# Moving the weight splits of a mixture-of-experts gate/up stage into the branch that uses them

## The chip, the cores and the metric

The kernel runs on one core of a Trainium2 chip. The metric is the device time of one execution in microseconds (us), the median of three runs. The engines are TensorE (PE in the profile; PEld is its weight load), VectorE (DVE), ScalarE (ACT), GpSimd (POOL) and SyncE (SP), whose queue issues most of the transfers from HBM.

## The reference

Two decoder layers over 256 tokens of width 1024. Each has a mixer (sparse attention, a convolution and a state-space group), a feed-forward part and a gated per-layer embedding. The feed-forward part of the second layer is the one that the change touches: eight experts, of which every token takes two.

```
def swiglu(x, w1, w3, w2):
    return (jax.nn.silu(x @ w1) * (x @ w3)) @ w2

def moe_swiglu(x, router, w1, w3, w2):
    logits = (x @ router).astype(jnp.float32)
    top_vals, top_idx = lax.top_k(logits, TOP_K)
    wts = jax.nn.softmax(top_vals, axis=-1)
    comb = jnp.einsum('blk,blke->ble', wts, jax.nn.one_hot(top_idx, N_EXPERTS, dtype=jnp.float32))
    y = jnp.zeros(x.shape, jnp.float32)
    for e in range(N_EXPERTS):
        y = y + comb[..., e:e + 1] * swiglu(x, w1[e], w3[e], w2[e])
    return y.astype(x.dtype)
```

w1 and w3 of an expert are 1024 x 3584, w2 is 3584 x 1024, all float32.

## The kernel before

The kernel computes only the tokens that an expert was given. `gather` collects them into `xe`, `expert` runs the three matrix products, and the result is scattered back (`sc`) and added to `y`. The 3584 columns are taken in four **chunks** (three of 1024, one of 512). An expert needs 42 loads of 1 MB each: 28 for w1 and w3 (eight per chunk of 1024, four for the last chunk) and 14 for w2, the down product. All loads of all experts stand in one list; `feed` issues the next one on SP's queue (L269) as soon as one of 13 buffers of 1 MB is free, so a transfer starts when the reader of an earlier load has let go of its buffer.

How many tokens an expert got is known only when the kernel runs. `either` therefore writes each load's matmuls twice, in two arms of an If on the count `n`:

```
            with self.tc.If(n > SM) as many:
                emit(False)
            with many.Else():
                emit(True)
            self.give()
        self.flush()
```

SM is 64. In the arm for at most 64 tokens (called **few** here) PE multiplies the raw float32 weights (L1537), with two halves of the columns in two halves of the array. In the other arm (**many**) each product is made of three faster matmuls (`mm3`, L334 to L336) from a high and a low part of the weights: ScalarE writes the high part (`split`, L339), VectorE the rest (L340), two pairs of instructions per load, into four buffers `whl`. These splits stand ahead of the If, in `split = list(self.parts(w, ku, cw))`, whatever the arm. For w2 both arms use the raw weights (L1573) and there is no split. `n` is loaded into a register of PE alone, so PE alone takes the branch; on the other engines each If is an empty block.

After a chunk `gate` follows: ScalarE's Silu of the first product (`hb`, L1496), VectorE's product with the second (`hb`, L1497), then PE's transposes (`hT`, L1507) and two copies out of PSUM (`ht`: ScalarE L1516, VectorE L1514). `flush` writes each of these steps behind a later load's If. VectorE also zeroes the halves of new accumulators (`mgu`, L1484). A scheduler then fixes the order on each engine, and may put whole Ifs of the next expert among those of this one's down product; every engine meets the Ifs in one and the same order.

Of the kernel before, what the change touches and what calls it, by code (L numbers as in the profile page):

```python
# [17 lines left out]
S = 256  # L18
# [136 lines left out]
RBN = 2  # L155
OV = 2
HB = 4
LOADS = 42
SM = 64
OVF = 6  # L160
# [33 lines left out]
class Trunk:  # L194
# [64 lines left out]
    def feed(self):  # L259


        while self.slots and self.nspec < len(self.specs):
            pool, tag, n = slot = self.slots.pop(0)
            if slot == self.over and OVF * LOADS <= self.nspec and self.kept is not None:
                self.kept.append(slot)
            elif pool is not self.xp or self.nspec < (NE - 1) * LOADS:
                src, a, b = self.specs[self.nspec]
# [21 lines left out]
    def parts(self, raw, a, b, low=None):  # L289
# [3 lines left out]
        for i0 in range(0, a, step):  # L293
            m = min(step, a - i0)
            n = m * b
            flat = raw[:, i0 : i0 + m].rearrange("p a b -> p (a b)")
            both = self.st.tile([P, 2, 1024], F32R, tag="hl", name="whl", bufs=HB)
            hi, lo = both[:, 0, :n], both[:, 1, :n]
# [269 lines left out]
    def square_parts(self, order, raw, low):  # L568
# [3 lines left out]
        for n, k in enumerate(order):  # L572
            if n % 2 == 0:
                both = self.st.tile([P, 2, D], F32R, tag="hl", name="whi", bufs=HB)
            hi = both[:, n % 2]
# [20 lines left out]
    def mixer(self, l, mp):  # L596
# [17 lines left out]
        def kv_columns():  # L614
# [8 lines left out]
            for ku in range(4):  # L623
                if ku == 2:
                    yield kv
                for kk, wh, wl in self.stream(w[:, 2 * ku : 2 * ku + 2, 512:1304], 2, 792):
# [3 lines left out]
                    if late:  # L630

                        held.append((k, wh, wl))
                        if k < HB - 1:
                            continue
# [651 lines left out]
    def moe(self, l, mp):  # L1286
        nc, a, sm = self.nc, self.a, self.sm
# [80 lines left out]
        cint = mp.tile([1, 1 + NE], I32, name="cint")  # L1368
# [20 lines left out]
        def pair(e):  # L1389

            advance(self.gather(th, tl, [one_hot(e, tt) for tt in range(TT)], S, GT))

        for e in range(NE):
            if e == OVF:

                while self.todo:
                    self.flush()
                self.ring, self.nload = self.kept, 0
                self.overflow(j, mp, Da[:, e // 2 % 2], cint, th, tl, rank, sel, comb, y)
                self.slots, self.kept = self.slots + self.kept, None  # L1400
                self.feed()
                pair(e)
            Dm = Da[:, e // 2 % 2]
            es = ts(e % 2)
            De = [Dm[:, tt, e % 2] for tt in range(TT)]
            D2 = mp.tile([P, TT, P], F32, tag="D2", name="D2")
            for tt in range(TT):
                nc.vector.tensor_scalar(D2[:, tt], slots, rank2[:, tt, e : e + 1], sel[:, tt, e : e + 1], op0=ALU.is_equal, op1=ALU.mult)
            ce = [comb[:, tt, e : e + 1] for tt in range(TT)]
            n = nc.tensor.value_load(cint[0:1, e + 1 : e + 2], min_val=0, max_val=S)  # L1410
            ahead = (lambda: pair(e + 1)) if e % 2 and e + 1 not in (OVF, NE) else None
            last = e == NE - 1
            late = self.ple_early(l, mp) if last else None
            self.expert(mp, None, n, self.xh[:, :, es], De, [D2[:, tt] for tt in range(TT)], ce, y, ahead, norm if last else None, late)
            if e == NE - 2:

                lnp = self.ln_params(l, 1, mp, "tl")
                bias = self.ple_bias(l, mp.tile([P, D], F32, tag="h2", name="gb"), mp.tile([P, D], F32R, tag="th", name="gbr"))
# [51 lines left out]
    def expert(self, mp, loads, n, xe, Dm, D2, comb, y, ahead=None, done=None, late=None):  # L1470
# [3 lines left out]
        nc = self.nc  # L1474
# [5 lines left out]
        def pair(name):  # L1480
            acc = self.pair(name)
            if n is not None:
                for h in range(2):
                    nc.vector.memset(acc[h][rows[1 - h]], 0.0)  # L1484
            return acc
# [6 lines left out]
        def gate(ci, hw, accs):  # L1492
            hbs = []
            for h in range(2):
                hb = mp.tile([P, 512], F32, tag="hb", name="hb", bufs=2)
                nc.scalar.activation(hb[:, :hw], accs[0][h][:, :hw], AF.Silu)  # L1496
                nc.vector.tensor_mul(hb[:, :hw], hb[:, :hw], accs[1][h][:, :hw])  # L1497
                hbs.append(hb)
            self.todo.append(lambda: turn(ci, hw, hbs))
# [22 lines left out]
        for ci, (c0, cw) in enumerate(CHUNKS):  # L1522
            hw, ku = cw // 2, 2048 // cw
            accs = []
            for wi in range(2):
                acc = pair("mgu")
                for u in range(KT // ku):
                    w = get()
                    split = list(self.parts(w, ku, cw))

                    def emit(few):
                        for i, wh, wl in split:
                            k = u * ku + i
                            for h in range(2):
                                hs = slice(h * hw, (h + 1) * hw)
                                if few:
                                    mm(acc[h][rows[h], :hw], xe[:, k, 0:SM], w[:, i, hs], start=k == 0, stop=k == KT - 1)  # L1537
                                else:
                                    self.mm3(acc[h][:, :hw], xs[:, 0, k], xs[:, 1, k], wh[:, hs], wl[:, hs], k == 0, k == KT - 1)

                    self.either(n, emit)
                accs.append(acc)
            if ci == 0:

                def turn_slots():

                    ps = self.tr("DT")
                    for i, src in enumerate([v.bitcast(F32) for v in Dm] + D2):
                        nc.tensor.transpose(ps[:, i * P : (i + 1) * P], src, self.ident)

                    def out():
                        t = mp.tile([P, 2, TT, P], F32R, tag="DT", name="DT", bufs=1)
                        nc.scalar.activation(t.rearrange("p h t s -> p (h t s)"), ps, AF.Copy)
                        DT.append(t)

                    self.todo.append(out)

                self.todo.append(turn_slots)
            self.todo.append(lambda ci=ci, hw=hw, accs=accs: gate(ci, hw, accs))
        acc = pair("mo")  # L1560
        NK = D_FFE // P
        for g in range(NK // 2):
            if late:
                next(late, None)
            w = get()

            def emit(few):
                for i in range(2):
                    k = 2 * g + i
                    ht, hf = hts[k]  # L1570
                    for h in range(2):
                        dst, x = (acc[h][rows[h]], ht[:, rows[hf]]) if few else (acc[h], ht)
                        mm(dst, x, w[:, i, h * 512 : (h + 1) * 512], start=k == 0, stop=k == NK - 1)  # L1573

            self.either(n, emit)
            if g == 3 and ahead:
                ahead()
# [202 lines left out]
```

## Time and profile before

| | us |
|---|---|
| time, median of 3 runs (lowest, highest) | 1639.78 (1639.73, 1644.44) |
| the profiled execution's own time | 1649.05 |
| its span, first to last instruction | 1647.3 |
| in it: eight experts, 629.7 to 1605.9 | 976.2 |

The page gives the busy time of each engine over the whole span: PE 1433.5 us (87%), VectorE 1195.0 us (73%), ScalarE 859.8 us (52%). These shares are means over stages with different limits, so what counts here is read expert by expert.

### The profile page before, as it was taken

Reading aid. Unit: us, or ns where it says so; the run is one execution under the profiler, and the core shown is the slowest. Engines: PE = TensorE matmul, PEld = TensorE weight load, DVE = VectorE, ACT = ScalarE, POOL = GpSimd, SP = SyncE. Lnnn points to the kernel's source line nnn. Section 1 sums busy time; section 2 is a strip of 40 time slices with the busy share of each in tenths; the row PEclk is TensorE's granted clock in tenths of the full one; section 3 lists DMA queues with packets and bytes.
Section 4 is the critical chain, followed back from the end, with each engine's and each line's share of the span. In section 5 each row is a group of like instructions: output and inputs, shape, how many; then the busy total and the mean of one; then the engine's idle time right before and its main releaser. Section 6 shows DMA issues by size and latency. Waiting matters only on the chain. (4 is left out here: it accounts for less than half of the span.)

```text
span 1647.3 us, 19143 instructions
## 1 busy us (share of the span) xinstructions
PE 1433.5 (87%) x6702; PEld 900.9 (55%) x6703; DVE 1195.0 (73%) x1564; ACT 859.8 (52%) x1175; POOL 261.4 (16%) x202
## 2 busy tenths in 40 slices
PE   6776999998987787798799998799999998688797
PEld 6544788876764473242347833347756843233245
DVE  7989558647679868968848837859736906967956
ACT  5454455434464536846536535647535705755742
POOL 4755107503044401000000000000000000001030
PEclk9797999999997798889899999899999999789898
DMA  6431465553542166999999989999979996999971
GB/s 244 150 132 39 155 202 184 172 191 134 179 136 102 51 249 262 370 365 409 404 342 404 364 283 381 361 351 405 374 268 352 368 309 241 352 372 394 402 315 51
DMA packets 139649, 445.56 MB, mean 270 GB/s; under 512 B 7408, under 2 KB 19312, under 8 KB 138496
## 3 DMA queue, kind: packets, MB, share of 16 engines
q1 hardware_dynamic: 138496, 437.42, 71.8%
q0 software_dynamic: 1024, 6.38, 1.1%
q8 instruction: 86, 1.41, 0.3%
q14 instruction: 43, 0.35, 0.1%
HBM read 442.72 MB, written 1.05 MB: 269 GB/s over the span
## 5 line engine op out<-in xcount | busy, mean ns | idle before, releaser
L340 DVE TENSOR_TENSOR whl<-wraw,whl 128x1024 fp32r<-128x1024 f32 (+2 forms) x557 | 661.2, 1227 | 178.0 <-ACT whl L339 173.4
L339 ACT ACTIVATE whl<-wraw 128x1024 fp32r<-128x1024 f32 (+2 forms) x557 | 565.1, 1041 | 312.8 <-DMA wraw<-in_moe_w_dram 73.2
L1537 PE MATMUL mgu<-wraw,xe 128*64 128x512 f32 (+1 forms) x1280 | 276.7, 583 | 13.3 <-DMA wraw<-in_moe_w_dram 5.5
L1573 PE MATMUL mo<-wraw,ht 128*64 128x512 f32 (+1 forms) x896 | 276.5, 598 | 0.0
L1537 PEld LDWEIGHTS mgu<-wraw,xe 128*64 128x64 f32 x1280 | 98.3, 149 | 179.7 <-issue 165.8
L1573 PEld LDWEIGHTS mo<-wraw,ht 128*64 128x64 f32 (+1 forms) x896 | 104.3, 158 | 148.3 <-issue 144.8
L334 PE MATMUL mgu<-whl,xs 128*128 128x512 f32 (+1 forms) x384 | 145.5, 379 | 6.1 <-DVE mgu L1484 5.0
L336 PE MATMUL mgu<-whl,xs 128*128 128x512 f32 (+1 forms) x384 | 140.4, 366 | 0.5 <-DVE whl L340 0.5
L335 PE MATMUL mgu<-whl,xs 128*128 128x512 f32 (+1 forms) x384 | 139.9, 364 | 0.0
L536 POOL DMA_DIRECT2D lnp<-in_lnp_dram x5 | 2.8, 565 | 799.0 <-ACT xe L1446 758.1
L1507 PE MATMUL hT<-sqr,hb 128*128 128x128 f32 x224 | 41.7, 342 | 80.0 <-DVE hb L1497 79.9
L334 PEld LDWEIGHTS mgu<-whl,xs 128*128 128x128 f32 x384 | 72.5, 189 | 27.6 <-DVE mgu L1484 7.5
L1507 PEld LDWEIGHTS hT<-sqr,hb 128*128 128x128 f32 x224 | 33.4, 176 | 97.1 <-ACT whl L339 63.7
L335 PEld LDWEIGHTS mgu<-whl,xs 128*128 128x128 f32 x384 | 72.6, 189 | 13.0 <-issue 1.7
L340 DVE TENSOR_TENSOR ot<-mo,ot 128x512 fp32r<-128x512 f32 x16 | 10.6, 688 | 95.2 <-ACT ot L339 95.1
L336 PEld LDWEIGHTS mgu<-whl,xs 128*128 128x128 f32 x384 | 72.4, 189 | 13.1 <-DVE whl L340 1.0
L1484 DVE MEMSET mgu<- 64x512 f32 x128 | 62.1, 485 | 21.6 <-issue 7.6
L336 PE MATMUL fffn_w<-whl,xh 128*128 128x512 f32 (+1 forms) x192 | 72.1, 375 | 0.0
L335 PE MATMUL fffn_w<-whl,xl 128*128 128x512 f32 (+1 forms) x192 | 71.8, 374 | 0.0
L334 PE MATMUL fffn_w<-whl,xh 128*128 128x512 f32 (+1 forms) x192 | 71.4, 372 | 0.0
L339 ACT ACTIVATE ot<-mo 128x512 fp32r<-128x512 f32 x16 | 9.0, 596 | 113.4 <-PE mo L1573 113.4
L1497 DVE TENSOR_TENSOR hb<-hb,mgu 128x512 f32<-128x512 f32 (+1 forms) x64 | 36.6, 612 | 27.1 <-PE mgu L335 14.8
(374 smaller groups left out, 2358.5 us busy)
## 6 DMA issues: line engine op xcount, KB each, us to landing
wraw<-in_moe_w_dram SPq DMA_DIRECT2D x336, 1024.0 KB, 7.9
wraw<-in_ffn_w_dram SPq DMA_DIRECT2D x33, 1024.0 KB, 5.1
wraw<-in_cmp_w_dram SPq DMA_DIRECT2D x8, 1024.0 KB, 5.4
wraw<-in_w_out_dram SPq DMA_DIRECT2D x8, 1024.0 KB, 7.0
wraw<-in_ple_gate_w_dram SPq DMA_DIRECT2D x8, 1024.0 KB, 7.2
wraw<-in_w_in_dram SPq DMA_DIRECT2D x8, 792.0 KB, 6.3
wraw<-in_w_in_dram SPq DMA_DIRECT2D x8, 768.0 KB, 7.0
lnp<-in_lnp_dram POOLq DMA_DIRECT2D x5, 1024.0 KB, 5.7
```

The source lines that it names most:

```text
L334: mm(dst, xh, wh, start=start, stop=False)
L335: mm(dst, xl, wh, start=False, stop=False)
L336: return mm(dst, xh, wl, start=False, stop=stop)
L339: h = self.hi = self.nc.scalar.activation(dh, src, AF.Copy)
L340: return h, (low or self.nc.vector).tensor_tensor(dl, src, dh.bitcast(F32), op=ALU.subtract)
L536: (queue or self.nc.gpsimd).dma_start(t.rearrange("p a d -> p (a d)"), self.a["lnp"][l, i : i + 1, :].to_broadcast([P, 2 * D]))
L1484: nc.vector.memset(acc[h][rows[1 - h]], 0.0)
L1497: nc.vector.tensor_mul(hb[:, :hw], hb[:, :hw], accs[1][h][:, :hw])
L1507: nc.tensor.transpose(pss[h][:, i * P : (i + 1) * P], hbs[h][:, i * P : (i + 1) * P], self.ident)
L1537: mm(acc[h][rows[h], :hw], xe[:, k, 0:SM], w[:, i, hs], start=k == 0, stop=k == KT - 1)
L1573: mm(dst, x, w[:, i, h * 512 : (h + 1) * 512], start=k == 0, stop=k == NK - 1)
```

## The change

The list of splits ahead of the If goes; `emit` makes the splits itself, in the many arm only. So that ScalarE and VectorE can skip them, the count is loaded into a register of those two engines as well (`values_load` with three engines), and with that every If of every expert, those of the down product too, becomes a compare and a branch on three engines instead of one.

```
+BRANCH = (mybir.EngineType.PE, mybir.EngineType.Activation, mybir.EngineType.DVE)
...
-            n = nc.tensor.value_load(cint[0:1, e + 1 : e + 2], min_val=0, max_val=S)
+            n = nc.values_load(cint[0:1, e + 1 : e + 2], engines=BRANCH, min_val=0, max_val=S)
...
                     w = get()
-                    split = list(self.parts(w, ku, cw))
 
                     def emit(few):
-                        for i, wh, wl in split:
+                        for i, wh, wl in [(i, None, None) for i in range(ku)] if few else self.parts(w, ku, cw):
                             k = u * ku + i
                             for h in range(2):
                                 hs = slice(h * hw, (h + 1) * hw)
```

The lines of the changed kernel stand one higher. The order of instructions moves with it. On ScalarE, at the end of the first chunk of the first expert (the pattern is the same in the other chunks and experts), the splits of the loads that arrive on DMAHW7 and then DMAHW0 stand before the change so:

```order
L339 ACTIVATE whl<-wraw 128x1024 [waits DMAHW7_49,DVE_49,PE_49]
L339 ACTIVATE whl<-wraw 128x1024 [waits DVE_49,PE_49]
L339 ACTIVATE whl<-wraw 128x1024 [waits DMAHW0_49,DVE_49,PE_49]
L339 ACTIVATE whl<-wraw 128x1024 [waits DVE_49,PE_49]
L1463 UNCONDITIONAL_BRANCH
L1516 ACTIVATE ht<-hT 128x512 [waits PE_49]
```

and in the changed kernel so:

```order
L340 ACTIVATE whl<-wraw 128x1024 [waits DVE_49,DMAHW7_49,PE_49,Activation_49]
L340 ACTIVATE whl<-wraw 128x1024
L1464 UNCONDITIONAL_BRANCH
L1464 UNCONDITIONAL_BRANCH [waits Activation_49]
L1517 ACTIVATE ht<-hT 128x512 [waits PE_49]
L1464 COMPARE_AND_BRANCH
L340 ACTIVATE whl<-wraw 128x1024 [waits DMAHW0_49,DVE_49,Activation_49]
L340 ACTIVATE whl<-wraw 128x1024
L1464 UNCONDITIONAL_BRANCH
L1464 UNCONDITIONAL_BRANCH [waits Activation_49]
```

The splits are now framed by a compare-and-branch and two jumps (the second is the few arm, which is empty but for a wait), and the copy `ht`, which waits for PE's transposes, stands ahead of the splits of the load on DMAHW0 instead of behind them. On PE, at the same place, the transposes stand before the change between the loads on DMAHW6 and DMAHW7:

```order
L1537 MATMUL mgu<-wraw,xe 64x512 [waits DMAHW6_49,DVE_49]
L1537 MATMUL mgu<-wraw,xe 64x512 [waits DVE_49]
L1537 MATMUL mgu<-wraw,xe 64x512 x2
L1463 UNCONDITIONAL_BRANCH
L1507 MATMUL hT<-sqr,hb 128x128 [waits DVE_49]
L1507 MATMUL hT<-sqr,hb 128x128 x3
L1507 MATMUL hT<-sqr,hb 128x128 [waits DVE_49,Activation_49]
L1507 MATMUL hT<-sqr,hb 128x128 x3
L1463 COMPARE_AND_BRANCH
```

and in the changed kernel one load later, between DMAHW7 and DMAHW0:

```order
L1537 MATMUL mgu<-wraw,xe 64x512 [waits DMAHW7_49]
L1537 MATMUL mgu<-wraw,xe 64x512 x3
L1464 UNCONDITIONAL_BRANCH
L1508 MATMUL hT<-sqr,hb 128x128 [waits DVE_49]
L1508 MATMUL hT<-sqr,hb 128x128 x3
L1508 MATMUL hT<-sqr,hb 128x128 [waits DVE_49,Activation_49]
L1508 MATMUL hT<-sqr,hb 128x128 x3
L1464 COMPARE_AND_BRANCH
```

Before, the transposes came before the block of the load on DMAHW7 and the copies that read them behind the splits of DMAHW0. After, transposes, copies and the splits of DMAHW0 follow upon one another. VectorE's order, shown here from the changed kernel, has the same sequence with its own work in front (`mgu` are the zeroed halves):

```order
L1498 TENSOR_TENSOR hb<-hb,mgu 128x512 [waits DVE_49,PE_49]
L1485 MEMSET mgu 64x512 [waits DVE_49] x2
L1515 COPY ht<-hT 128x512 [waits PE_49]
L1464 COMPARE_AND_BRANCH
L341 TENSOR_TENSOR whl<-wraw,whl 128x1024 [waits DMAHW0_49,Activation_49]
L341 TENSOR_TENSOR whl<-wraw,whl 128x1024 [waits Activation_49]
L1464 UNCONDITIONAL_BRANCH
L1464 UNCONDITIONAL_BRANCH [waits DVE_49]
```

There too nothing of the load on DMAHW0 is split before the copy `ht` is done.

## Rows read from the trace of the kernel before

**Rows 1.** Busy time and count by line, operation and tile, whole span.
```profile
L340 DVE TENSOR_TENSOR whl<-wraw,whl 128x1024 fp32r<-128x1024 f32 (+2 forms) x557 | 661.2, 1227 | 178.0 <-ACT whl L339 173.4
L339 ACT ACTIVATE whl<-wraw 128x1024 fp32r<-128x1024 f32 (+2 forms) x557 | 565.1, 1041 | 312.8 <-DMA wraw<-in_moe_w_dram 73.2 <-PE mgu L336 60.2 <-PE fffn_w L336 44.9
L1537 PE MATMUL mgu<-wraw,xe 128*64 128x512 f32 (+1 forms) x1280 | 276.7, 583 | 13.3 <-DMA wraw<-in_moe_w_dram 5.5 <-DVE mgu L1484 4.3 <-DVE comb L1330 3.4
...
L336 PE MATMUL mgu<-whl,xs 128*128 128x512 f32 (+1 forms) x384 | 140.4, 366 | 0.5 <-DVE whl L340 0.5
```
**Rows 2.** One stretch per expert: us, busy PE PEld DVE ACT POOL, PEclk, DMA share, GB/s.
```profile
629.70:749.40 119.70, 97.00 (x443) 38.99 (x443) 94.73 (x112) 73.83 (x83) 0.00 (x0) 0.89 0.94 360
749.40:866.30 116.90, 98.85 (x457) 43.92 (x456) 86.72 (x98) 65.44 (x74) 0.00 (x0) 0.93 0.99 384
866.30:999.60 133.30, 130.91 (x522) 85.03 (x522) 86.93 (x99) 66.68 (x72) 0.00 (x0) 0.99 0.96 352
999.60:1113.80 114.20, 96.75 (x457) 43.08 (x457) 86.93 (x99) 65.45 (x74) 0.00 (x0) 0.94 0.96 364
1113.80:1248.10 134.30, 132.12 (x537) 91.25 (x537) 86.28 (x96) 66.99 (x72) 0.00 (x0) 1.00 0.94 348
1248.10:1370.40 122.30, 120.36 (x485) 81.72 (x484) 68.27 (x77) 52.58 (x57) 0.00 (x0) 1.00 0.90 321
1370.40:1503.00 132.60, 102.48 (x476) 44.98 (x477) 102.80 (x116) 79.55 (x89) 2.54 (x4) 0.87 0.93 348
1503.00:1605.90 102.90, 88.10 (x398) 35.32 (x398) 83.13 (x89) 63.76 (x73) 16.89 (x10) 0.93 0.94 369
```
**Rows 3.** PE in order of time, first expert (few): start, us, what, idle before.
```profile
633.68 13.95 PE L1537 MATMUL mgu<-wraw,xe 128*64 128x512 f32 x64
654.39 1.97 PE L1507 MATMUL hT<-sqr,hb 128*128 128x128 f32 x8 [6.76 <-DVE hb L1497]
656.29 14.43 PE L1537 MATMUL mgu<-wraw,xe 128*64 128x512 f32 x64
677.01 1.94 PE L1507 MATMUL hT<-sqr,hb 128*128 128x128 f32 x8 [6.28 <-DVE hb L1497]
```
**Rows 4.** VectorE in order of time, one chunk of the first expert.
```profile
660.18 5.74 DVE L340 TENSOR_TENSOR whl<-wraw,whl 128x1024 fp32r<-128x1024 f32 x5
...
676.19 1.27 DVE L1497 TENSOR_TENSOR hb<-hb,mgu 128x512 f32<-128x512 f32 x2
677.38 3.48 DVE L340 TENSOR_TENSOR whl<-wraw,whl 128x1024 fp32r<-128x1024 f32 x3
680.79 0.68 DVE L1514 COPY ht<-hT 128x512 f32<-128x512 f32 x1
```
**Rows 5.** Stretches of steady work, columns as in rows 2.
```profile
1500.00:1590.00 90.00, 75.67 (x342) 31.45 (x344) 70.48 (x80) 62.06 (x72) 3.42 (x2) 0.92 1.03 404
1110.00:1175.00 65.00, 62.52 (x288) 50.64 (x287) 59.84 (x66) 47.76 (x50) 0.00 (x0) 1.00 1.03 404
...
880.00:926.00 46.00, 46.00 (x210) 37.92 (x210) 44.28 (x47) 36.94 (x39) 0.00 (x0) 1.00 1.02 387
1365.00:1392.00 27.00, 21.27 (x96) 11.95 (x97) 17.79 (x26) 13.20 (x16) 0.60 (x1) 0.87 0.64 229
```
**Rows 6.** DMA issues: size of one, us from issue to landing.
```profile
wraw<-in_moe_w_dram SPq DMA_DIRECT2D x336, 1024.0 KB, 7.9
```
**Rows 7.** PE in order of time, second expert, down product.
```profile
816.61 1.94 PE L1573 MATMUL mo<-wraw,ht 128*64 128x512 f32 x8
...
819.26 1.95 PE L1537 MATMUL mgu<-wraw,xe 128*64 128x256 f32 x16
```
**Rows 8.** ScalarE in order of time, third expert (many).
```profile
904.04 1.06 ACT L339 ACTIVATE whl<-wraw 128x1024 fp32r<-128x1024 f32 x1 [0.31 <-PE mgu L336]
905.42 1.06 ACT L339 ACTIVATE whl<-wraw 128x1024 fp32r<-128x1024 f32 x1 [0.31 <-PE mgu L336]
906.79 1.06 ACT L339 ACTIVATE whl<-wraw 128x1024 fp32r<-128x1024 f32 x1 [0.31 <-PE mgu L336]
907.75 0.58 ACT L1516 ACTIVATE ht<-hT 128x512 f32<-128x512 f32 x1
```
**Rows 9.** PE in order of time, third expert: transposes of two chunks.
```profile
906.59 1.03 PE L1507 MATMUL hT<-sqr,hb 128*128 128x128 f32 x8
929.53 1.03 PE L1507 MATMUL hT<-sqr,hb 128*128 128x128 f32 x8
```

More of the change, by code (lines that the diff above doesn't have):

```diff
@@ L157 @@
 HB = 4
+BRANCH = (mybir.EngineType.PE, mybir.EngineType.Activation, mybir.EngineType.DVE)
 LOADS = 42
@@ L1409, in moe @@
             ce = [comb[:, tt, e : e + 1] for tt in range(TT)]
-            n = nc.tensor.value_load(cint[0:1, e + 1 : e + 2], min_val=0, max_val=S)
+            n = nc.values_load(cint[0:1, e + 1 : e + 2], engines=BRANCH, min_val=0, max_val=S)
             ahead = (lambda: pair(e + 1)) if e % 2 and e + 1 not in (OVF, NE) else None
@@ L1528, in expert @@
                     w = get()
-                    split = list(self.parts(w, ku, cw))
                     def emit(few):
-                        for i, wh, wl in split:
+                        for i, wh, wl in [(i, None, None) for i in range(ku)] if few else self.parts(w, ku, cw):
                             k = u * ku + i
```

## The prediction

> **What bounds the kernel now.** I first read the groups by line, to see how much work the change touches. ScalarE's 557 split instructions take 565.1 us and VectorE's 557 take 661.2 us [rows 1]; both counts hold the 448 of the experts (56 pairs in each of eight) and some of earlier stages. In the few arm these parts are read by nobody: there PE takes the raw weights.
>
> Next come the stretches, one per expert [rows 2]. They show two kinds. In three, the third, fifth and sixth, PE is busy for 130.91 of 133.30 us, 132.12 of 134.30 and 120.36 of 122.30: those are the many arms, and PE's matmuls set the time. In the other five PE is busy for 97 of 120 us or so. Those are the few arms, with a DMA share of 0.93 to 0.99. It would be easy to stop here and call them bound by transfers. But the best steady rate shown is 404 GB/s at a share of 1.03 [rows 5], and the first few expert moved only 360 [rows 2]. So there are gaps, and the order of time must say who makes them.
>
> It does for the first expert. PE runs a chunk's 64 matmuls in 13.95 us without waiting, then stands still for 6.76 us, next time 6.28 us, and the releaser is VectorE's `hb` [rows 3]. VectorE meanwhile runs split behind split, five in 5.74 us, and comes to `hb` when its queue lets it [rows 4]. From transposes to transposes PE needs 677.01 - 654.39 = 22.6 us per chunk. So the gate/up stage of a few expert is held by VectorE, through splits that nobody reads.
>
> What is the next limit? A load is 1024.0 KB [rows 6], 1.0486 million bytes, and at 404 GB/s takes 2.60 us. Eight loads of a chunk take 20.8 us, the 42 of an expert 109.2 us.
>
> **What is removed.** Five few experts lose 5 x 56 = 280 pairs: 280 x 1.041 = 291 us of ScalarE and 280 x 1.227 = 344 us of VectorE, by the means of [rows 1]. Nearly all of that is off the path, since behind VectorE stands the transfer queue. A chunk goes from 22.6 us to the larger of 20.8 (transfers) and PE's 13.95 + 1.97 = 15.9 [rows 3], plus a short wait for the Silu and product, which the pause of PE between loads covers. The gain is 22.6 - 20.8 = 1.8 us a chunk, 3.5 chunks, 6.3 us an expert. The last few expert (102.90 us, and 404 GB/s over most of it [rows 2, 5]) is at the floor already. Four experts give 25 us; as the first chunk partly lives on loads that came early, I take **24**.
>
> Bounds, by the floor: the stretches of 119.7, 116.9, 114.2 and 132.6 us lie 10.5, 7.7, 5.0 and 23.4 above 109.2 [rows 2]. From the last I take off the pause at 1365 to 1392, with 229 GB/s over 27 us [rows 5], 27 x (1 - 229/404) = 11.7, which a check between experts makes. Sum 34.9, so at most **35**. From below: the idle DMA shares are 0.06, 0.01, 0.04 and 0.07 of these stretches [rows 2], 7.2 + 1.2 + 4.6 + 9.3 = 22, less the pause's 0.36 x 27 = 9.7: **12**.
>
> **What is moved.** In the many arms the splits stay, 84 loads, but may no longer run ahead of an If. The chunks of 1024 repeat every 929.53 - 906.59 = 22.94 us [rows 9], 1.03 of it transposes, so a load's matmuls take 21.9 / 8 = 2.74 us. PE is busy in 46.00 of 46.00 us there, VectorE in 44.28 [rows 5], so VectorE has 0.86 us to spare per chunk, no more. ScalarE even waits 0.31 us for PE before each split [rows 8]: it is ahead.
>
> After the change the transposes, the copies `ht` and the splits of the next load stand one behind the other, with no matmuls of PE in between (the order in the section on the change). ScalarE can copy after the first half of the transposes, 0.52 us; its copy takes 0.58 and a split 1.06 [rows 8], so the first high part is there at 2.16, where PE was done at 1.03 [rows 9]: a wait of 1.13. Each of the load's twelve matmuls takes 2.74 / 12 = 0.23 us; PE does the two that need the high part alone, 0.46, until 2.62; the third needs the low part, which VectorE gives at 2.16 + 1.2 = 3.36 [rows 1]: another 0.74. Together 1.9 us per chunk end. The fourth turn lies in the down product, which has no splits, so it is three per expert, nine in all: **17 us** lost. Bounds: if only the high part is missed, 1.13 x 9 = **10**. VectorE's view is worse: it idles from its last low part over PE's last four matmuls (0.92), the transposes (1.03) and from its copy's end (0.68 [rows 4]) to the split at 3.08 (0.45), 2.4 us in all, of which 0.86 is spare. That is 1.5, near the 1.9 of PE, so both engines lose the same time; without the spare, 2.4 x 9 = **22**.
>
> A second order effect I cost at nothing: ScalarE's splits of a load now wait at once for the whole block of PE two loads back, where they waited half by half. The 0.31 us waits show that it has the time, and where it is late the price is in the upper bound.
>
> **What is added.** Each If is a compare and a branch on ScalarE and VectorE. The trace shows no such instruction on them. From below nothing: VectorE's five splits take 1.148 us each across the jumps of empty Ifs [rows 4], and PE, which branches already, needs 1.74 us per load over eight Ifs [rows 3], no more than the 1.94 of a single one [rows 7]. From above I take ScalarE's 0.31 us [rows 8], the nearest pause between two neighbours on such an engine: 84 x 0.31 = 26 us. It is nearest to the jumps and to PE's branch, so I take nothing; VectorE, with the 2.4 us stalls counted, has some 0.04 us per load left as cover in the many arms. In the few arms and in the down products both engines have nothing to do, and transfers hide the branch, as they hide PE's own pauses: PE works 1.94 and 1.95 us on blocks that start 2.65 us apart [rows 7]. The register loads, one per engine and expert, stand where PE waited for the count anyway.
>
> [...]
>
> **Sum.** The profiled run took 1649.05 us for its 1647.3 us span and lies 9.3 us above the median of the runs, 1639.8. 1649.05 - 24 + 17 = 1642; less those 9.3, 1632.8 on the scale of the median. I take **1632**.
>
> **The rivals.**
> *The many arms lose nothing.* If the 13 buffers let a late gate/up stage be made up in the down product, whose blocks of 1.74 to 1.94 us are shorter than a load, only the gain is left: 1639.8 - 24 = 1616, with the floor's 35 it is 1605. For it: the DMA share in many experts is 0.90 to 0.96 [rows 2]. Against it: PE works in 98% of their time, so what it loses has nowhere to be made up.
> *Slower: the branch is exposed on VectorE.* Place: every split load of the many arms. At 0.31 us less 0.04 of cover, 84 x 0.27 = 23 us, and 1632 + 23 = 1655. It decides from (7 / 84) + 0.04 = 0.12 us per branch; from 0.18 the kernel is slower by more than 0.3%. For it: VectorE has 44.28 of 46 us filled [rows 5]. Against it: PE's own branches don't show.
> *Little happens.* The few arms gain only the idle DMA share, 12, and the stalls cost 17: 1639.8 - 12 + 17 = 1645. For it: the second expert already runs at 384 GB/s and a share of 0.99 [rows 2]. Against it: the 6 us waits of every chunk [rows 3].
>
> **How the numbers follow.** 0.3% of 1640 is 4.9 us, about what this measurement can tell from no change. My forecast, 1632 (own range 1624 to 1640), has 0.42; two thirds of it is faster, one third the same. The many arms unhurt: 0.18, all faster. The branch exposed: 0.20, nearly all slower. Little happens: 0.20, half the same, half slower. So faster 0.46, same 0.25, slower 0.29. The range goes from 1608, within the first rival, to 1658, just beyond the second.
>
> **What would show it.** Right: in few experts no PE wait for `hb` of over 2 us, chunks of 20.8 us, 400 GB/s; in many experts a PE wait of 1.1 and then 0.7 us behind `hT` at three chunk ends, chunks of 24.8 us. Wrong, if few stretches stay at 115 to 120 us, if many chunks stay at 22.9, or if each split on VectorE is followed by a pause of 0.1 us or more and PE waits for `whl` at every load.

## The result, and the profile after

The changed kernel takes 1655.26 us (median of four runs, 1654.95 to 1656.19) against 1641.3 beside it: ratio 1.0084, 95% interval 1.0066 to 1.0102. It is 14 us slower, where 8 us faster was forecast (1632 against 1639.8); the time lies inside the stated range, the direction is wrong.

The stretches, cut as in [rows 2] at each expert's last scatter, show both sides at once (columns as there):

```profile
620.80:733.80 113.00, 91.73 (x443) 34.24 (x443) 23.58 (x52) 11.42 (x19) 0.00 (x0) 0.90 0.98 379
733.80:851.50 117.70, 94.99 (x457) 43.03 (x456) 32.92 (x50) 18.15 (x26) 0.00 (x0) 0.91 0.97 377
851.50:995.20 143.70, 134.72 (x521) 86.05 (x521) 77.82 (x91) 56.01 (x64) 0.00 (x0) 0.98 0.89 324
995.20:1105.80 110.60, 92.95 (x457) 41.59 (x456) 33.16 (x51) 18.15 (x26) 0.00 (x0) 0.94 0.98 378
1105.80:1254.70 148.90, 140.08 (x536) 95.23 (x536) 86.57 (x96) 64.02 (x73) 0.00 (x0) 0.95 0.86 313
1254.70:1388.90 134.20, 125.81 (x484) 83.95 (x484) 73.34 (x81) 53.86 (x61) 0.00 (x0) 0.97 0.84 301
1388.90:1512.40 123.50, 96.53 (x477) 40.13 (x477) 26.09 (x48) 12.28 (x21) 2.54 (x4) 0.88 0.98 378
1512.40:1612.50 100.10, 82.05 (x398) 33.73 (x398) 34.37 (x45) 20.45 (x29) 16.88 (x10) 0.93 0.95 374
```

Line by line against [rows 2], the five few experts change by -6.7, +0.8, -3.6, -9.1 and -2.8 us, together -21.4. The three many experts change by +10.4, +14.6 and +11.9, together +36.9. VectorE is indeed relieved, from 94.73 to 23.58 us busy in the first expert, and still the stage is 15.5 us longer. Two more things are to be seen in the many lines: PE is idle for 8 to 9 us of each where it was idle for about 2, and its granted clock, 0.99 and twice 1.00 before, is 0.98, 0.95 and 0.97.

A little is gained ahead of these stretches, which begin with the first expert's first matmul. From the router's first product (`lg`) to that matmul the kernel before takes 23.9 us (605.78 to 629.71) and the changed one 21.3 (599.50 to 620.78). The other kernels below with the splits ahead of the If take 23.6 to 24.0 us there, those with the splits in the arm 21.0 to 21.3. With these 2.6 us the balance is 36.9 - 21.4 - 2.6 = 12.9, near the 14 of the medians.

PE in order of time at one chunk end of the third expert, which answers to [rows 9], shows both:

```profile
899.33 1.03 PE L1508 MATMUL hT<-sqr,hb 128*128 128x128 f32 x8
901.62 0.50 PE L335 MATMUL mgu<-whl,xs 128*128 128x512 f32 x1 [1.25 <-ACT whl L340]
901.96 0.39 PE L336 MATMUL mgu<-whl,xs 128*128 128x512 f32 x1
902.88 0.50 PE L337 MATMUL mgu<-whl,xs 128*128 128x512 f32 x1 [0.53 <-DVE whl L341]
...
903.73 0.63 PE L337 MATMUL mgu<-whl,xs 128*128 128x512 f32 x1
904.16 0.63 PE L335 MATMUL mgu<-whl,xs 128*128 128x512 f32 x1
...
906.72 0.54 PE L335 MATMUL mgu<-whl,xs 128*128 128x512 f32 x1
907.10 0.39 PE L336 MATMUL mgu<-whl,xs 128*128 128x512 f32 x1
```

The two waits behind the transposes are there as forecast, 1.25 for ScalarE and 0.53 for VectorE. What was not forecast stands below them: from 903.73 the matmuls follow at 0.43 us instead of 0.23 until 907.1. That is half speed: the granted clock of this stretch is 0.50, where from 899 to 903 us it was 1.00:

```profile
904.00:907.00 3.00, 3.00 (x8) 2.33 (x8) 2.23 (x2) 0.41 (x1) 0.00 (x0) 0.50 0.04 10
```

ScalarE and VectorE at the same place:

```profile
900.03 0.60 ACT L1517 ACTIVATE ht<-hT 128x512 f32<-128x512 f32 x1 [3.93 <-PE hT L1508]
900.52 3.89 ACT L340 ACTIVATE whl<-wraw 128x1024 fp32r<-128x1024 f32 x4
907.01 2.01 ACT L340 ACTIVATE whl<-wraw 128x1024 fp32r<-128x1024 f32 x2 [2.60 <-PE mgu L337]
```
```profile
900.40 0.69 DVE L1515 COPY ht<-hT 128x512 f32<-128x512 f32 x1 [0.83 <-PE hT L1508]
901.60 4.63 DVE L341 TENSOR_TENSOR whl<-wraw,whl 128x1024 fp32r<-128x1024 f32 x4 [0.50 <-ACT whl L340]
```

ScalarE idles 3.93 us until the transposes let its copy go, and only then comes to the splits that PE waits for. Further waits of this kind stand at the start of the same expert, behind the last scatter, and in mid-chunk:

```profile
853.10 0.50 PE L335 MATMUL mgu<-whl,xs 128*128 128x512 f32 x1 [1.63 <-ACT whl L340]
856.02 0.79 PE L337 MATMUL mgu<-whl,xs 128*128 128x512 f32 x1 [2.18 <-DVE whl L341]
916.03 0.50 PE L337 MATMUL mgu<-whl,xs 128*128 128x512 f32 x1 [0.28 <-DVE whl L341]
```

At the start ScalarE's first split begins at 852.00, behind its copy `DT`, which waits for the scatter. In the kernel before the first blocks were split earlier: there ScalarE's next split stands only at 870.76. Behind the third chunk there is no such wait. Its transposes stand behind the last matmul of gate/up, and the down product that follows needs no splits; so the order shown for the first chunk is not the same in every chunk:

```profile
930.81 1.04 PE L1508 MATMUL hT<-sqr,hb 128*128 128x128 f32 x8
```

The groups of PE by line for the third expert (busy, mean ns, idle before) add the waits up, of after and then of before:

```profile
L335 PE MATMUL mgu<-whl,xs 128*128 128x512 f32 (+1 forms) x112 | 41.9, 376 | 4.1 <-ACT whl L340 4.1
L337 PE MATMUL mgu<-whl,xs 128*128 128x512 f32 (+1 forms) x112 | 41.9, 380 | 4.3 <-DVE whl L341 4.3
```
```profile
L334 PE MATMUL mgu<-whl,xs 128*128 128x512 f32 (+1 forms) x112 | 41.9, 374 | 1.8 <-DVE mgu L1484 1.8
L336 PE MATMUL mgu<-whl,xs 128*128 128x512 f32 (+1 forms) x112 | 40.8, 364 | 0.0
```

8.4 us of waits against 1.8; the other two many experts have 8.2 and 8.1 against 1.6 each. So waits explain 24.7 - 5.0 = 19.7 of the 36.9 us. In the third expert they are 3.8 us at the start (1.8 before), 3.5 at the two chunk ends and 1.1 in mid-chunk. Most of the other 17 is half speed: the clock's shortfall, 0.02 x 143.7 + 0.05 x 148.9 + 0.03 x 134.2 less the 0.01 x 133.3 of before, comes to about 13 us.

### The profile page after: what moved, and what is told of

The parts are those of the page before. It is cut to its first block, busy times and chain, and to the rows that moved or that the text cites. A ratio compares the mean times of both kernels' runs of the same rounds, so it can differ in the third digit from the quotient of the medians.

```text
span 1652.7 us, 19521 instructions
## 1 busy us (share of the span) xinstructions
PE 1417.1 (86%) x6702; PEld 888.8 (54%) x6703; DVE 880.2 (53%) x1284; ACT 576.0 (35%) x895; POOL 261.4 (16%) x202
## 5 line engine op out<-in xcount | busy, mean ns | idle before, releaser
L341 DVE TENSOR_TENSOR whl<-wraw,whl 128x1024 fp32r<-128x1024 f32 (+2 forms) x277 | 334.3, 1237 | 184.2 <-ACT whl L340 183.2
L340 ACT ACTIVATE whl<-wraw 128x1024 fp32r<-128x1024 f32 (+2 forms) x277 | 275.1, 1029 | 247.3 <-DMA wraw<-in_moe_w_dram 55.5
L1537 PE MATMUL mgu<-wraw,xe 128*64 128x512 f32 (+1 forms) x1280 | 256.0, 549 | 48.2 <-DMA wraw<-in_moe_w_dram 41.1
L1537 PEld LDWEIGHTS mgu<-wraw,xe 128*64 128x64 f32 x1280 | 92.5, 138 | 200.3 <-issue 134.9
L335 PE MATMUL mgu<-whl,xs 128*128 128x512 f32 (+1 forms) x384 | 150.1, 392 | 44.9 <-ACT whl L340 44.9
L337 PE MATMUL mgu<-whl,xs 128*128 128x512 f32 (+1 forms) x384 | 147.0, 388 | 12.5 <-DVE whl L341 12.4
L336 PE MATMUL mgu<-whl,xs 128*128 128x512 f32 (+1 forms) x384 | 144.8, 379 | 0.0
L335 PEld LDWEIGHTS mgu<-whl,xs 128*128 128x128 f32 x384 | 76.0, 198 | 67.7 <-ACT whl L340 53.3
L1497 ACT ACTIVATE hb<-mgu 128x512 f32<-128x512 f32 (+1 forms) x64 | 33.2, 543 | 191.9 <-PE mgu L1537 162.0
L1517 ACT ACTIVATE ht<-hT 128x512 f32<-128x512 f32 (+1 forms) x32 | 17.4, 544 | 220.2 <-PE hT L1508 220.2
L337 PEld LDWEIGHTS mgu<-whl,xs 128*128 128x128 f32 x384 | 74.7, 197 | 34.2 <-DVE whl L341 21.6
L336 PEld LDWEIGHTS mgu<-whl,xs 128*128 128x128 f32 x384 | 76.0, 198 | 14.1 <-issue 1.7
L984 DVE SCALAR_TENSOR_TENSOR cy<-upad,pk,cy 128x256 f32<-128x256 f32 x60 | 54.7, 912 | 1.1
```

Source lines behind the costliest of these rows:

```text
L335: mm(dst, xh, wh, start=start, stop=False)
L336: mm(dst, xl, wh, start=False, stop=False)
L337: return mm(dst, xh, wl, start=False, stop=stop)
L340: h = self.hi = self.nc.scalar.activation(dh, src, AF.Copy)
L341: return h, (low or self.nc.vector).tensor_tensor(dl, src, dh.bitcast(F32), op=ALU.subtract)
L984: nc.vector.scalar_tensor_tensor(y0, u(0, k), w(0, k), y0, op0=ALU.mult, op1=ALU.add)
```

## The experiments

Theory: the loss is the order of the splits in the many arms, with half-speed matmuls as its consequence; the gain of the few arms is real. Rivals: the branch on ScalarE and VectorE costs the time; the few arms were held by transfers.

**The branch alone.** The changed kernel with the splits put back ahead of the If:

```
                     w = get()
+                    split = list(self.parts(w, ku, cw))
 
                     def emit(few):
-                        for i, wh, wl in [(i, None, None) for i in range(ku)] if few else self.parts(w, ku, cw):
+                        for i, wh, wl in split:
```

> The three engines branch, but the splits stay ahead of the If as before the change. Theory (the loss is the order of the splits in the many arms, and half-speed matmuls after the waits that it makes): nothing is lost, 1637 to 1646 us, as the kernel before. Rival (the branch itself costs time on VectorE and ScalarE): at 0.1 us a branch the 224 split loads, which VectorE has no spare for, add 22 us, 1663; and if the whole loss of the many experts, 37 us in the traces, were the branch, 1678 or more.

Measured: 1643.74 us against 1643.47, ratio 1.0000 (0.9987 to 1.0014). All 336 Ifs (eight experts of 42 loads) branch on three engines and nothing is lost, even in the few chunks where VectorE has no spare (from 655 to 690 us no pause of it is longer than 0.18 us): from transposes to transposes they take 674.60 - 651.99 = 22.61 us, as in [rows 3].

```profile
651.99 1.97 PE L1508 MATMUL hT<-sqr,hb 128*128 128x128 f32 x8 [7.79 <-DVE hb L1498]
674.60 1.94 PE L1508 MATMUL hT<-sqr,hb 128*128 128x128 f32 x8 [5.10 <-DVE hb L1498]
```

The branch falls as a cause. In this run the arms of ScalarE and VectorE are empty; where they hold the splits, in the changed kernel, VectorE's four splits of two loads take 4.63 us in the row shown above, 1.16 each as against 1.15 in [rows 4], so the branch between them does not show either. All of the 14 us comes from where the splits stand.

**All experts in one arm.** The condition of the If is replaced, in the kernel before and in the changed one (and with it the threshold up to which an expert's slots are doubled); for all few it is `n > 2 * P`:

```
-            with self.tc.If(n > SM) as many:
+            with self.tc.If(n > 0) as many:
```

> The kernel before with the condition set to n > 0 (and the doubled slots of small experts left out with it), so that all eight experts take the many arm. Only a base for the next run: by the three many experts' stretches, 134.3, 133.3 and 122.3, against 117.3 in the mean of the five others, about 5 x 13 = 65 us over the kernel before, 1705 us.

> The changed kernel with the same condition. Theory (37 us lost in three many experts, 12 each): 8 x 12 = 98 us over the base, 1803. The recorded prediction's term (1.9 us at each chunk end, no more): 8 x 5.7 = 46 us over the base, 1751.

> The kernel before with a condition that is never true, so that all eight experts take the few arm; tokens past the 64th of three experts are left out or mixed up. A base for the next run: 3 x 13 us under the kernel before, about 1600 us, and VectorE's hb the releaser of PE's waits in every expert.

> The changed kernel with the condition that is never true; the same tokens are left out. Theory (gain of few experts up to the transfers' pace, some 5 us each): 8 x 5 = 40 us under the base, 1560, with a DMA share of 0.97 or more in each expert. Rival (the few arms were held by transfers already): 15 us or less under the base.

All many: 1772.78 us before, 1869.42 after: 96.6 us for eight experts, 12.1 each, as the stretches said (36.9 / 3 = 12.3) and twice the recorded 5.7. The base itself was put 68 us too low, and the one with all experts few 39 too high: the stretches of a mixed run [rows 2] are no measure of a run of one kind.

All few: 1561.23 before, 1540.49 after: 20.7 us, half of the 40 expected, and more than the rival's 15. The stretches say why. Three experts in the middle of the run, of before and then of after:

```profile
854.20:965.80 111.60, 86.84 (x408) 35.49 (x409) 85.83 (x99) 64.36 (x72) 0.00 (x0) 0.91 1.02 401
965.80:1074.50 108.70, 91.35 (x440) 38.56 (x440) 86.94 (x99) 65.44 (x74) 0.00 (x0) 0.94 1.02 399
1074.50:1186.80 112.30, 88.26 (x409) 34.53 (x408) 85.09 (x96) 64.24 (x72) 0.00 (x0) 0.91 1.02 400
```
```profile
841.40:950.60 109.20, 83.41 (x409) 31.96 (x409) 22.64 (x43) 8.94 (x16) 0.00 (x0) 0.91 1.03 404
950.60:1059.80 109.20, 87.65 (x441) 35.92 (x440) 23.70 (x43) 10.14 (x18) 0.00 (x0) 0.92 1.03 403
1059.80:1169.00 109.20, 83.36 (x409) 32.32 (x408) 21.86 (x40) 8.94 (x16) 0.00 (x0) 0.91 1.03 404
```

After, each is at the floor of 109.2 us worked out in the prediction. But before they took 110.9 in the mean, at 400 GB/s, although PE waits as in [rows 3] there too (an order of time in the first of these stretches):

```profile
890.08 1.94 PE L1507 MATMUL hT<-sqr,hb 128*128 128x128 f32 x8 [7.34 <-DVE hb L1497]
```

A wait of 7 us on PE that costs next to nothing, 1.7 us an expert with all its like: from 867 to 913 us, across two such waits, the transfers move 404 GB/s. The likely reason is this: gate/up is too slow by 1.8 us a chunk, 6 us an expert, which is two to three loads; buffers that came free in the down product take those, and the transfers go on. And what PE no longer waits for `hb` it waits for a transfer later on, among the blocks of the down product. So it does in the first two experts of the change itself. The first row's wait was 2.96 us before the change; the splits that the second row waits for had in turn waited for their load:

```profile
706.62 3.68 PE L1537 MATMUL mgu<-wraw,xe 128*64 128x512 f32 x8 [20.04 <-DMA wraw<-in_moe_w_dram]
818.58 0.80 PE L335 MATMUL mgu<-whl,xs 128*128 128x512 f32 x1 [17.86 <-ACT whl L340]
```

By this reading the wait for `hb` costs time where the buffers are full already, as in the first expert, for which 13 loads were issued before it began. Its transfers, 90 us of before and of after, in the kernels of the change itself:

```profile
640.00:730.00 90.00, 68.19 (x324) 27.83 (x322) 76.83 (x85) 59.80 (x68) 0.00 (x0) 0.87 0.97 376
```
```profile
630.00:720.00 90.00, 69.70 (x354) 26.55 (x352) 16.49 (x31) 7.27 (x13) 0.00 (x0) 0.89 1.02 399
```

**The copies out of the way.** If the order is the cause, another order must give the time back. First the copies `ht` of the first three chunks are written into both arms of the next load's If:

```
...
+                def copies():
+                    nc.scalar.activation(ht[:, :nb].rearrange("p k t -> p (k t)"), pss[0][:, :hw], AF.Copy)
+                    nc.vector.tensor_copy(ht[:, nb:].rearrange("p k t -> p (k t)"), pss[1][:, :hw])
+                armed.append(copies)
+                return
...
+                        split = [(i, None, None) for i in range(ku)] if few else list(self.parts(w, ku, cw))
+                        for f in now:
+                            f()
```

> The changed kernel with the two copies ht of the first three chunks written into both arms of the next load's If, behind its splits, so that the splits no longer stand behind the transposes. Theory: the two waits of 1.20 and 0.53 us behind the transposes go at two chunk ends of three experts, 10 us, and about 6 us of half-speed matmuls with them: 1655 - 16 = 1639 us (1635 to 1646), chunks of about 23.5 us. Rival (the branch costs the time): 1655, chunks stay at 25.7 to 27.3 us.

Measured: 1648.14 us, ratio to the kernel before 1.0029 (1.0014 to 1.0044). The gain is half of what was expected. PE and VectorE at the chunk end show what was missed:

```profile
874.50 1.03 PE L1509 MATMUL hT<-sqr,hb 128*128 128x128 f32 x8
...
877.45 0.50 PE L337 MATMUL mgu<-whl,xs 128*128 128x512 f32 x1 [1.46 <-DVE whl L341]
```
```profile
875.57 0.69 DVE L1517 COPY ht<-hT 128x512 f32<-128x512 f32 x1 [0.90 <-PE hT L1509]
876.18 4.62 DVE L341 TENSOR_TENSOR whl<-wraw,whl 128x1024 fp32r<-128x1024 f32 x4
```

ScalarE's wait is gone, but within the arm the scheduler left VectorE's copy ahead of its splits, so the wait moved there. The next kernel gives both copies to ScalarE:

```
-                    nc.vector.tensor_copy(ht[:, nb:].rearrange("p k t -> p (k t)"), pss[1][:, :hw])
+                    nc.scalar.activation(ht[:, nb:].rearrange("p k t -> p (k t)"), pss[1][:, :hw], AF.Copy)
```

> The kernel with the copies in the arms, and both copies on ScalarE behind its splits, so that VectorE's splits of the next load no longer wait for the transposes either (in the run before, the wait behind them had moved to VectorE's part, 1.46 us at two chunk ends of three experts). Theory: that wait and the half-speed matmuls behind it go, 6 x 1.46 = 9 us and some 3 more, 1648 - 12 = 1636 us (1632 to 1642). Rival (what is left is the wait for a whole block or the branch, in every load): 1646 to 1650, as before.

Measured: 1640.04 us, ratio 0.9986 (0.9974 to 0.9998), inside the theory's bounds. The three many stretches are 138.1, 141.1 and 129.0 us, 18.6 less than the 426.8 of the change: so much does the sequence of transposes, copies and splits cost. 18.3 above the kernel before are left; 8.4 of them are idle time of PE, at the starts and in mid-chunk. The clock goes with the waits, place by place. In the third expert, the stretch with the two chunk ends had 0.97 after the change (first row). Here it has 1.00 (second row), and only the start, where waits of 1.63 and 2.19 us have stayed, is below (third row):

```profile
870.00:930.00 60.00, 55.41 (x267) 44.98 (x266) 49.65 (x51) 37.24 (x41) 0.00 (x0) 0.97 0.88 324
```
```profile
870.00:930.00 60.00, 58.92 (x283) 47.17 (x281) 53.11 (x56) 45.07 (x52) 0.00 (x0) 1.00 0.97 361
855.00:870.00 15.00, 11.65 (x40) 9.09 (x41) 12.55 (x15) 8.48 (x10) 0.00 (x0) 0.77 1.02 411
```

**The splits one load ahead.** On top of the first of these two, the arm of a load makes the splits of the next load (`nxt`, taken from the list one load ahead):

```
...
+                        if few:
+                            split = [(i, None, None) for i in range(ku)]
+                        else:
+                            split = parted.pop(0) if parted else list(self.parts(w, ku, cw))
+                            if nxt:
+                                parted.append(list(self.parts(nxt[0], *nxt[2])))
```

> The kernel of the run with the copies in the arms, and in the many arm of a load the splits of the next load are made, so that the splits run one load ahead again, as they could before the change. Theory: nearly all of the 37 us lost in the many experts comes back, the gain of the few experts stays: 1655 - 30 = 1625 us (1617 to 1634), faster than both kernels. Rival (branch): 1650 or more.

Measured: 1634.76 us, ratio 0.9946 (0.9924 to 0.9967): faster than both kernels, a little past the expected bounds. Its many stretches:

```profile
851.00:987.80 136.80, 132.44 (x522) 84.93 (x522) 74.70 (x89) 55.57 (x63) 0.00 (x0) 0.99 0.90 336
1099.00:1236.50 137.50, 133.30 (x537) 91.06 (x537) 85.59 (x96) 65.93 (x72) 0.00 (x0) 1.00 0.90 334
1236.50:1362.50 126.00, 121.76 (x485) 81.48 (x484) 69.92 (x79) 53.43 (x59) 0.00 (x0) 1.00 0.88 323
```

With the waits the half speed is gone: 0.99 and twice 1.00, the same as before the change. 10 us of the 36.9 are still lost. 6.3 of them are idle time of PE: 0.28 us in mid-chunk as before, and new waits between the two halves of the transposes (0.27, 0.71 and 0.66 us in the third expert), for VectorE does splits between its two products `hb`:

```profile
918.30 0.63 PE L1516 MATMUL hT<-sqr,hb 128*128 128x128 f32 x4 [0.66 <-DVE hb L1506]
```

> The kernel with the splits one load ahead, and both copies on ScalarE. Theory: the waits behind the transposes are gone already, so it stays within 4 us of 1635. Rival (VectorE still sets the pace of the many arms): 5 us or more faster.

Measured with both copies on ScalarE: 1632.86 us, ratio 0.9955 (0.9939 to 0.9972), no different from the kernel with the splits ahead. So VectorE's copies do not set the pace there.

## Why the prediction was wrong

**What bounds the kernel.** That PE waits for `hb` in the few arms was read rightly, and that these waits hold the stage was read wrongly: by the argument above they hold it only where the buffers are full, and elsewhere PE waits for transfers later on instead (17.86 us, by way of the splits, in the second expert of the changed kernel). In the second expert the prediction had the row for it, a DMA share of 0.99 [rows 2], and used it for a rival alone.

**What is removed: 24.** The stretches gave 21.4, and 2.6 more lie ahead of them. That the sum is right is luck, for its parts are not: four equal gains of 6.3 were forecast, and they came as 6.7, -0.8, 3.6, 9.1 and 2.8. Nor did chunks of 20.8 us come: the first expert's follow after 14.9 us (transposes at 640.10 and 655.01), and the transfers' pace shows as one wait of 20.04 us behind them. The rival "little happens", with the transfers as the limit, describes the second expert before the change and, in the run with all experts few, the middle ones.

**What is added: nothing.** Right: the run with the branch alone gives 1.0000, within 0.14%. So the rival with the exposed branch, 23 us more, falls. It had named 1655 us, the time that was measured; that its number came true, and that the range which it widened holds the result, is luck.

**What is moved: 17.** This is the step that failed, by its size: 36.9 us. The single chunk end held: its waits were put at 1.13 and 0.74 and measured 1.20 to 1.25 and 0.53. Their number did not: they stand at two chunk ends of each expert, not three, so 10.5 us of waits in all. With the half speed behind them this sequence is worth 18.6 us by the run with both copies on ScalarE; that this is near 17 is luck. What was missing is the other 18. The prediction said that the splits "may no longer run ahead of an If", and priced that at the chunk ends alone; the rest stood under "a second order effect I cost at nothing". But PE also waits at the start of each many expert (1.63 and then 1.85 to 2.18 us, where 1.6 to 1.8 were before) and in mid-chunk (0.28, 0.53). The price of half-speed matmuls behind a wait was in no term. "PE works in 98% of their time, so what it loses has nowhere to be made up" held: the down products gave nothing back (in the third expert, from the transposes of `DT` to the last scatter, 52.6 us before and after).

What stays open: some 4 of the last 10 us in the many experts of the kernel with the splits ahead, and about 4 of the 36.9 that neither waits nor the clock account for. That half speed follows from the waits is shown by their going together, place by place, in the last kernels, not by a run that adds a wait alone. That a full set of buffers makes the wait for `hb` cost time is argued from the first expert; no run changed the number of buffers.

## What to carry to other kernels

The splits that moved into an arm of the If lost their freedom to run ahead, on ScalarE and on VectorE, at 36.9 us in three experts; before such a move, look in the order of the new kernel at what stands directly ahead of the work in each place where it used to be early: at starts and in mid-stage as well as at the ends. An engine's wait can cost far less than its length: PE's wait of 7.34 us for `hb` cost, with all its like, 1.7 us an expert where all experts were few. Ask whether the transfers pause during it before it is put into a sum. And where an arm must make its own operands, make those of the next arm in it: that kept the gain here (1634.76 against 1643.47 us) and gave back most of the loss.

## What the runs showed of the hardware

Two waits of 1.25 and 0.53 us amid dense matmuls were followed by 3 us of matmuls at a granted clock of 0.50 (0.43 against 0.23 us apart). It is not so at every such place: the same expert's earlier chunk end, with waits of 1.20 and 0.53, went on at a clock of 1.00 (875 to 885 us, 0.23 us apart). Compares and branches of 336 Ifs on ScalarE and on VectorE did not show in the time (ratio 1.0000, 0.9987 to 1.0014).
